# One-core hybrid decoder layer: key/value weights and transposed x loaded as one tile per k step, and three places re-ordered

## The chip, the cores and the metric

The kernel runs on one core of a Trainium2 chip. The metric is device time in microseconds (us), the median over runs of the same kernel. The engines are TensorE (PE: matmuls, PEld: its weight loads), VectorE (DVE), ScalarE (ACT), GpSimd (POOL) and SyncE (SP, which issues most DMA transfers). Each engine works its own queue of instructions in order and waits on semaphores of the others.

## The reference

One decoder layer in fp32, 256 tokens by 2048 channels, for batch 1 and depth 1:

```python
h = rmsnorm(x, norm_mix_pre[l])
proj = h @ w_in[l]
xr, yr, q, k, v, g_rnn, g_attn = jnp.split(proj, IN_OFFSETS, axis=-1)
xr = causal_depthwise_conv(xr, conv_w[l], conv_b[l])
xr = rg_lru(xr, positions, w_rg_a[l], b_rg_a[l], w_rg_x[l], b_rg_x[l], lru_lambda[l])
y_rnn = xr * jax.nn.gelu(yr)
q = rope(q.reshape(B, S, N_Q_HEADS, HEAD_DIM), positions)
k = rope(k.reshape(B, S, N_KV_HEADS, HEAD_DIM), positions)
v = v.reshape(B, S, N_KV_HEADS, HEAD_DIM)
y_att = sliding_window_sink_attention(q, k, v, attn_sinks[l])
mix = jax.nn.sigmoid(g_rnn) * (y_rnn @ w_rnn_proj[l]) + jax.nn.sigmoid(g_attn) * (y_att @ w_attn_proj[l])
x = x + rmsnorm(mix @ w_out[l], norm_mix_post[l])
h = rmsnorm(x, norm_mlp_pre[l])
u = jnp.square(jax.nn.relu(h @ w_mlp_up[l]))
x = x + rmsnorm(u @ w_mlp_down[l], norm_mlp_post[l])
```

There are 32 query heads and 4 key/value heads of 64 channels, so k and v together are 512 columns, and the MLP is 8192 wide. Attention runs in blocks of 128 tokens: the first block sees 128 keys, the second 256, under a mask and with one sink logit per head.

## The kernel before

Every matmul is built from three: each fp32 operand is split into a high part, which ACT casts (`hi`, `whi`), and a low part, which DVE subtracts (`lo`, `wlo`), and the products high x high, high x low and low x high are summed in one PSUM bank (128 x 512). One 512-wide product of the emulated kind is thus three matmuls of 512 columns.

Weights come through the class `Stream`. SP loads them in order as halves of 128 x 1024 (512 KB) into a ring of four tiles (`wraw`, WRAW = 4). ACT's cast and DVE's subtraction write rings of six (`whi`, `wlo`, WHALF = 6), and the matmuls take the halves by `half()`, which also keeps loads and splits a fixed number of halves ahead. For some pairs of halves, `SEVEN`, the MLP uses seven products over sums of blocks instead of eight. The Tile framework puts semaphores between engines; `pin` keeps marked instructions in program order, and the rest is scheduled by priority.

**Opening.** The program order of the loads is `w_kv` (8 halves, two k tiles of 512 columns each) mixed with x transposed (`x_t`: 256, 256 and three times 512 KB) on SP, and a small tile of constants `tiny` (105 KB, with the norm's gain `gcol`) on ACT's queue. Ten halves (`EXTRA`) lie in larger tiles of a pool with twelve places, so that 14 halves are loaded before any place in the ring must come free: the eight of `w_kv` and six of the gates. `split_first` splits the first half in two pieces; `part(k)` makes the high part of x times gain on ACT and the low part on DVE; `kv_step(j)` issues the matmuls of two k tiles into two banks `kv` (L415). Ahead of it stand 20 warm-up matmuls (L396). The tokens' scaling by the norm is applied later. After the opening the gate weights `w_g` follow (PE `g`, L307 to L311).

**Attention.** Attention of a key/value group g is a generator that yields between its steps, and the matmul loops of other work (`a_pair`, `b_pass512`) take one step from it every so many matmuls (`pump`). Its steps are scores, mask, maxima, `exponents` (ACT, L610), `shares` (DVE, scaling, L620), `turn_probs` (transposes on PE, `pt`, L636; copies to SBUF on ACT, L638), and the products with v (`po`, L678). A bank pool has two banks; `pt` uses the pool `psm`. The last group (g = 3) runs beside the matmuls `ps` with `hT` (L267, L269).

**Second norm.** The output projection of two token blocks (tb) by four quarters q of 512 columns ends in `o` banks. `gained` (DVE, L924, and ACT's squares, L921) and `scaled` by the norm (DVE, L967) make `h`, whose quarters PE transposes (`ptr`, L973), ACT casts to the high part of `h2T` (L978) and DVE subtracts to its low part (L983). Between the transposes of the second block stand the first matmuls of the MLP's up-projection (L1027), four or six at a time. ACT's queue holds the splits of the first weight halves of that projection (L116) there.

**Close.** The down-projection `down` of the last quarter pair sums 16 pairs of halves in four banks for (tb, n) = (0,0), (0,1), (1,0), (1,1). Two pairs are held back (`held` = 2) and done bank by bank at the end (L1134), each followed by `finish`: a sum on DVE (L1269), a square with row sum on ACT (L1270), a product with the gain on DVE (L1271). After a token block's last bank come the reduction (L1275), the root, the reciprocal, four scalings added to x (L1283) and the output transfers (L1284).

## Time and profile before

| what | us |
|---|---|
| median of 3 runs (1502.19 to 1502.8) | 1502.19 |
| the profiled execution | 1502.42 |
| its span in the trace | 1500.6 |
| PE busy | 1485.3 |
| DVE busy | 1097.8 |
| ACT busy | 829.6 |
| first real matmul starts (L415) | 7.43 |
| last matmul starts | 1490.58 |
| last reduction starts (L1275) | 1493.29 |

The profiled execution took 1.82 us more than its span, and 0.23 more than the median. The mean granted clock of PE over the span is 0.997 of full speed. DMA moved 199 GB/s over the span on the mean, and 339 in the first fortieth of it. A row of waits gives the engine and line that waited, what released it, the total in us, the number of times and the longest; a row of the timeline gives start, duration, engine, line, operation, tiles, count, and in square brackets the idle time before it and what ended it.

### The profile page before, as it was taken

Reading aid. Unit: us, or ns where it says so; the run is one execution under the profiler, and the core shown is the slowest. Engines: PE = TensorE matmul, PEld = TensorE weight load, DVE = VectorE, ACT = ScalarE, POOL = GpSimd, SP = SyncE. Lnnn points to the kernel's source line nnn. Section 1 sums busy time; section 2 is a strip of 40 time slices with the busy share of each in tenths; the row PEclk is TensorE's granted clock in tenths of the full one; section 3 lists DMA queues with packets and bytes.
Section 4 is the critical chain, followed back from the end, with each engine's and each line's share of the span. In section 5 each row is a group of like instructions: output and inputs, shape, how many; then the busy total and the mean of one; then the engine's idle time right before and its main releaser. Section 6 shows DMA issues by size and latency. Waiting matters only on the chain.

```text
span 1500.6 us, 19926 instructions
## 1 busy us (share of the span) xinstructions
PE 1485.3 (99%) x7568; PEld 1259.0 (84%) x7568; DVE 1097.8 (73%) x1356; ACT 829.6 (55%) x1137; POOL 1.7 (0%) x9
## 2 busy tenths in 40 slices
PE   9999999999999999999999999999999999999997
PEld 7887788788889888888889888888888888888886
DVE  6576668859669966555658866798886666788897
ACT  7564665647567665444355654555454555455453
POOL 0000000000000000000000000000000000000000
PEclk9999999999999999999999999999999999999999
DMA  8654554565646556555764765566667555566665
GB/s 339 217 161 156 166 163 136 169 195 172 210 155 211 179 200 208 184 191 188 276 216 144 262 190 192 186 208 206 210 204 242 189 193 187 192 239 210 204 215 186
DMA packets 83471, 298.28 MB, mean 199 GB/s; under 512 B 9264, under 2 KB 9520, under 8 KB 82352
## 3 DMA queue, kind: packets, MB, share of 16 engines
q1 hardware_dynamic: 80064, 289.57, 58.2%
q10 hardware_dynamic: 3312, 7.45, 1.4%
q8 instruction: 59, 0.97, 0.3%
q14 instruction: 36, 0.29, 0.1%
HBM read 290.69 MB, written 6.29 MB: 198 GB/s over the span
## 4 chain that ended last, share of the span: by engine, by line
PE 97%; DVE 2%; DMA 0%; ACT 0%; issue 0%; DVEq 0%; SPq 0%; ACTq 0%
PE ps L269 22%; PE ps L267 12%; PE dQ L1134 9%; PE s L1134 5%; PE dP L1134 4%; PE g L307 4%; PE g L311 4%; PE g L309 4%; PE pp L309 4%; PE pp L307 4%; PE pp L311 4%; PE dCs L1134 3%; PE q L307 2%; PE q L311 2%; PE q L309 2%; PE o L307 2%
## 5 line engine op out<-in xcount | busy, mean ns | idle before, releaser
L108 DVE TENSOR_TENSOR wlo<-wraw,whi 128x1024 fp32r<-128x1024 f32 x516 | 625.2, 1222 | 309.0 <-ACT whi L107 305.8
L107 ACT CAST whi<-wraw 128x1024 fp32r<-128x1024 f32 x516 | 537.8, 1051 | 546.5 <-PE ps L269 129.7
L269 PE MATMUL ps<-h2T,whi 128*128 128x512 f32 x960 | 223.9, 390 | 0.0
L269 PEld LDWEIGHTS ps<-h2T,whi 128*128 128x128 f32 x960 | 178.2, 188 | 35.7
L267 PEld LDWEIGHTS ps<-h2T,wlo 128*128 128x128 f32 x960 | 119.1, 192 | 2.3
L269 PE MATMUL ps<-hT,whi 128*128 128x512 f32 x512 | 120.7, 391 | 0.0
L267 PE MATMUL ps<-h2T,wlo 128*128 128x256 f32 x960 | 119.9, 283 | 0.0
L269 PEld LDWEIGHTS ps<-hT,whi 128*128 128x128 f32 x512 | 94.8, 188 | 20.3 <-issue 1.5
L1134 PE MATMUL dQ<-whi,uT 128*128 128x512 f32 x288 | 106.8, 389 | 0.0
L307 PE MATMUL g<-whi,hT 128*128 128x512 f32 x256 | 101.1, 395 | 0.0
L311 PE MATMUL g<-whi,hT 128*128 128x512 f32 x256 | 99.8, 390 | 0.0
L309 PE MATMUL g<-wlo,hT 128*128 128x512 f32 x256 | 99.8, 390 | 0.0
L267 PEld LDWEIGHTS ps<-hT,wlo 128*128 128x128 f32 x512 | 63.7, 192 | 1.2
L267 PE MATMUL ps<-hT,wlo 128*128 128x256 f32 x512 | 64.4, 283 | 0.0
L1134 PEld LDWEIGHTS dQ<-whi,uT 128*128 128x128 f32 x288 | 54.1, 188 | 11.2
L307 PEld LDWEIGHTS g<-whi,hT 128*128 128x128 f32 x256 | 48.1, 188 | 10.6 <-issue 1.0
L311 PEld LDWEIGHTS g<-whi,hT 128*128 128x128 f32 x256 | 48.0, 188 | 10.2
L309 PEld LDWEIGHTS g<-wlo,hT 128*128 128x128 f32 x256 | 48.1, 188 | 9.6
L1134 PE MATMUL dQ<-wlo,uT 128*128 128x512 f32 x144 | 56.0, 389 | 0.0
L1134 PE MATMUL dP<-whi,uT 128*128 128x512 f32 x144 | 54.1, 389 | 0.0
L1134 PE MATMUL dCs<-whi,uT 128*128 128x512 f32 x144 | 54.1, 389 | 0.0
L143 DVE TENSOR_TENSOR tlo<-t,thi 128x1536 fp32r<-128x1536 f32 x28 | 49.2, 1757 | 6.4 <-ACT thi L142 5.9
(284 smaller groups left out, 2464.5 us busy)
## 6 DMA issues: line engine op xcount, KB each, us to landing
wraw<-in_w_up SPq DMA_DIRECT2D x128, 512.0 KB, 4.1
wraw<-in_w_dn SPq DMA_DIRECT2D x128, 512.0 KB, 4.6
wraw<-in_w_g SPq DMA_DIRECT2D x64, 512.0 KB, 4.6
wraw<-in_w_xy SPq DMA_DIRECT2D x64, 512.0 KB, 4.6
wraw<-in_w_q SPq DMA_DIRECT2D x32, 512.0 KB, 4.4
wraw<-in_w_ap SPq DMA_DIRECT2D x32, 512.0 KB, 4.5
wraw<-in_w_rp SPq DMA_DIRECT2D x32, 512.0 KB, 3.8
wraw<-in_w_out SPq DMA_DIRECT2D x32, 512.0 KB, 5.1
```

The source lines that it names most:

```text
L107: self.pin(self.nc.scalar.copy(hi, src))
L108: self.pin(self.nc.vector.tensor_tensor(lo, src, hi.bitcast(F32), ALU.subtract))
L143: v.tensor_tensor(lo, t, hi.bitcast(F32), ALU.subtract)
L267: mm(ps[:, f, 1, :], w, a[:, 0, :], start=False, stop=j == 1 and k == 7)
L269: mm(ps[:, f].rearrange("p a b -> p (a b)"), w, a.rearrange("p a b -> p (a b)"), start=kt == 0, stop=j == 3 and k == 7)
L307: mm(banks[tb][n], a[:, 0, t], hi[:, n * 512 : n * 512 + 512], start=first, stop=False)
L309: mm(banks[tb][n], a[:, 0, t], lo[:, n * 512 : n * 512 + 512], start=False, stop=False)
L311: mm(banks[tb][n], a[:, 1, t], hi[:, n * 512 : n * 512 + 512], start=False, stop=last)
L1134: mm(b, a[x], w[y], start=not begun and i == 0, stop=tail and i == 2)
```

## The change

Four parts.

1. The opening. The key/value weights of one k tile (512 columns), x transposed of the same k tile (256), and, for the first, the norm's gain (16) lie side by side in memory, and each k tile is one transfer on SP: `kx_first` of 128 x 784 and fifteen `kx_rest` of 128 x 768. `tiny` goes to SP's queue behind the sixth. The split is per k tile (`kv_step(kt, hi, lo)`): a cast of 128 x 512 on ACT, of the first tile on DVE, the high and low part of x, the subtraction of 128 x 512, six matmuls. The stream's numbering starts at half 8 (`FIRST`), its large tiles are gone, so four gate halves are loaded before a place in the ring must come free, and not six.
2. Attention of the last group. One `yield` between its scores and masks, and one between the two `turn_probs(1, ...)`, are gone, one is added behind them; the transposes of the second pair part use the pool `psb`.
3. The second norm. `gained(1, 3)` and `scaled(1, 3)` come after `low(1, 0)`, and the third weight split of the up-projection after `high(1, 0)`.
4. The close. In the last `down` (`closing`) one more pair is worked first for the two banks of tb 0 only; its products for tb 1 are done at the end with the held pairs. The last bank (1,1) is done in two halves of 256 columns, the second in the free bank P1, with a fold of the partial sum on DVE (`fold`), and `finish` per half; sums of squares get five columns (`sq3`). The four scalings of tb 0 all come after (0,1), where before two came there and two after (1,0).

```diff
-EXTRA = 5
+FIRST = 8
...
-            if j < 2 * EXTRA:
-                if j % 2 == 0:
-                    self.place = self.room(f"wraw{j}")
-                t = self.place[:, c]
-            else:
-                t = self.pool.tile([P, 1024], F32, tag="wraw", bufs=WRAW, name=f"wraw{j}")
+            t = self.pool.tile([P, 1024], F32, tag="wraw", bufs=WRAW, name=f"wraw{j}")
...
+    kx, at = [], 0
+    for k in range(KT):
+        if k % 2 == 0:
+            place, at = flat(unit(f"kx{k}", F32)), 0
+        n = 512 + S + (KT if k == 0 else 0)
+        kx.append(place[:, at : at + n])
+        at += n
+        nc.sync.dma_start(kx[k], kx_rest[k - 1] if k else kx_first)
+        if k == 5:
+            nc.sync.dma_start(tiny, few)
+    gcol = kx[0][:, 512 + S :]
+    ws.load_to(FIRST + WRAW)
...
+    def kv_step(kt, hi, lo):
+        c, src = quarter(kt % 2), kx[kt][:, 0:512]
+        if kt:
+            pin(nc.scalar.copy(hi[:, c], src))
+        else:
+            pin(nc.vector.tensor_copy(hi[:, c], src))
+        part(kt)
+        pin(nc.vector.tensor_tensor(lo[:, c], src, hi[:, c].bitcast(F32), ALU.subtract))
+        for x, w in ((0, hi), (1, hi), (0, lo)):
+            for tb in range(TB):
+                pin(mm(kv[tb], hT[kt // 4][:, kt % 4, x, tb * P : tb * P + P], w[:, c],
+                       start=kt == 0 and w is hi and x == 0, stop=kt == KT - 1 and w is lo))
...
-                    ps = bank(psm, "pt")
+                    ps = bank(psb if last_group and tb and par else psm, "pt")
...
             three = scores(1, 1, [bank(psb, "sc") for par in range(2)])
-            yield
...
         turn_probs(1, (0,))
-        yield
+        if not last_group:
+            yield
         turn_probs(1, (1,))
         yield
+        if last_group:
+            yield
...
-    norm(1, lambda: low(0, 3), lambda: gained(1, 3, banks[1][1]))
-    for j in range(3):
+    norm(1, lambda: low(0, 3))
+    for j in range(2):
         begun.append(ws.split_high())
...
         high(1, q)
+        if q == 0:
+            begun.append(ws.split_high())
         low(1, q)
+        if q == 0:
+            gained(1, 3, banks[1][1])
+            scaled(1, 3)
...
+        def step(p, i, hi, lo, name, at=0, w=512, into=None):
+            tb, n2 = name
+            b = into or PLACE[name]
+            o = 0 if into else at
+            t = slice(tb * P, tb * P + P)
+            c = slice(n2 * 512 + at, n2 * 512 + at + w)
+            a = uT[p][:, i]
+            product(banks[b][:, o : o + w], (a[:, 0, t], a[:, 1, t]), (hi[:, c], lo[:, c]), b in begun,
+                    p == PAIRS - 1 and i == 1, w < 512 and not into)
+            begun.add(b)
...
+        if closing:
+            for i in range(2):
+                parts.append((PAIRS - held - 1, i) + ws.half())
+                for name in order[:2]:
+                    step(*parts[i], name)
...
+            if closing and k == 1:
+                a, r = order[-1], slice(256, 512)
+                fold = lambda: pin(v.tensor_tensor(ready[a][:, r], banks[PLACE[a]][:, r], ready[a][:, r], ALU.add))
+                for e in todo:
+                    step(*e, name)
+                finish(name, b, t, 0, 512, fold)
+            elif closing and k == 3:
+                for e in todo:
+                    step(*e, name, 0, 256)
+                finish(name, b, t, 0, 256)
+                for e in todo:
+                    step(*e, name, 256, 256, "P1")
+                finish(name, banks["P1"], t, 256, 256)
...
+            p = slice(at, at + w)
+            k = q + (at > 0)
+            pin(nc.vector.tensor_tensor(a[:, p], b[:, 0:w], t[:, p], ALU.add))
+            pin(nc.scalar.activation(spare[:, p], a[:, p], AF.Square, accum_out=sq3[:, tb, k : k + 1]))
+            pin(nc.vector.tensor_tensor(t[:, p], a[:, p], g3[:, q * 512 + at : q * 512 + at + w], ALU.mult))
             last[tb, i] = t
+            fold()
+            if at + w < 512:
+                return
...
-            for tb, qs in {(0, 1): ((0, (2, 0)),), (1, 0): ((0, (1, 3)),), (1, 1): ((1, (2, 0, 1, 3)),)}.get(name, ()):
+            for tb, qs in {(0, 1): ((0, (2, 0, 1, 3)),), (1, 1): ((1, (2, 0, 1, 3)),)}.get(name, ()):
```

At the opening, ACT's queue before, from its first transfer on (`wraw_80` holds w_kv, `xt_76` transposed x):

```order
L350 DMA tiny<-in_few 128x210
L377 ACT_TABLE_LOAD
L377 ACTIVATE st<-eps 128x1
L73 CAST whi_159<-wraw_80 128x512
L402 ACTIVATE hT_147<-xt_76,tiny 128x256
L73 CAST whi_159<-wraw_80 128x512
L402 ACTIVATE hT_147<-xt_76,tiny 128x256 x3
L116 CAST whi_185<-wraw_80 128x1024
L402 ACTIVATE hT_148<-xt_76,tiny 128x256 x2
L116 CAST whi_205<-wraw_86 128x1024
```

And ACT's queue after (`kx_77` holds k tiles 0 and 1):

```order
L350 ACT_TABLE_LOAD
L350 ACTIVATE st<-eps 128x1
L376 ACTIVATE hT_150<-kx_77 128x256
L385 CAST whi_162<-kx_77 128x512
L376 ACTIVATE hT_150<-kx_77 128x256
L385 CAST whi_184<-kx_80 128x512
L376 ACTIVATE hT_150<-kx_80,kx_77 128x256
L385 CAST whi_184<-kx_80 128x512
```

The first weight cast and the transfer of `tiny` have left ACT's queue, so that ACT begins with x; casts and parts of x now alternate one k tile at a time.

In the last group's attention, PE's queue before (`pt` is a transpose, L267 low and L269 high matmuls):

```order
L267 MATMUL ps<-hT_149,wlo_2311 128x256 x4
L267 MATMUL ps<-hT_150,wlo_2311 128x256 x4
L636 MATMUL pt<-ident,s 128x128 x8
L269 MATMUL ps<-hT_147,whi_2296 128x512 x3
...
L269 MATMUL ps<-hT_150,whi_2385 128x512 x4
L636 MATMUL pt<-ident,s 128x128 x8
L269 MATMUL ps<-hT_147,whi_2422 128x512
L267 MATMUL ps<-hT_147,wlo_2346 128x256 x4
L267 MATMUL ps<-hT_148,wlo_2346 128x256 x4
L267 MATMUL ps<-hT_149,wlo_2386 128x256
L636 MATMUL pt<-ident,s 128x128 x8
L267 MATMUL ps<-hT_149,wlo_2386 128x256 x3
```

And after (L248 low, L250 high matmuls, L609 transposes):

```order
L248 MATMUL ps<-hT_150,wlo_2217 128x256 x4
L248 MATMUL ps<-hT_151,wlo_2217 128x256 x4
L609 MATMUL pt<-ident,s 128x128 x8
L248 MATMUL ps<-hT_152,wlo_2283 128x256 x4
...
L248 MATMUL ps<-hT_153,wlo_2332 128x256 x4
L250 MATMUL ps<-hT_150,whi_2317 128x512 x3
L250 MATMUL ps<-hT_151,whi_2317 128x512 x4
L250 MATMUL ps<-hT_152,whi_2331 128x512 x4
L250 MATMUL ps<-hT_153,whi_2331 128x512 x4
L609 MATMUL pt<-ident,s 128x128 x16
L250 MATMUL ps<-hT_150,whi_2376 128x512 x4
```

The first eight transposes have moved ahead of 24 low matmuls, and the other two groups of eight, which had 10 matmuls between them, stand together.

In the second norm, DVE's queue before (L924 gains, L967 scalings, L983 low parts, L124 weight subtractions):

```order
L967 SCALAR_TENSOR_TENSOR h_6168<-h_6168,st,xg_6166 128x512 x3
L924 TENSOR_TENSOR h_6168<-o_6491,gpg_6160 128x512
L967 SCALAR_TENSOR_TENSOR h_6168<-h_6168,st,xg_6166 128x512
L983 TENSOR_TENSOR h2T_6177<-ptr_6753,h2T_6177 128x4x128
L983 TENSOR_TENSOR h2T_6178<-ptr_6754,h2T_6178 128x4x128
L124 TENSOR_TENSOR wlo_6874<-wraw_6676,whi_6820 128x1024
L983 TENSOR_TENSOR h2T_6179<-ptr_6753,h2T_6179 128x4x128
L983 TENSOR_TENSOR h2T_6180<-ptr_6754,h2T_6180 128x4x128
```

And after (L899, L932, L958, L105 in the same roles):

```order
L932 SCALAR_TENSOR_TENSOR h_6189<-h_6189,st,xg_6187 128x512 x3
L958 TENSOR_TENSOR h2T_6198<-ptr_6774,h2T_6198 128x4x128
L899 TENSOR_TENSOR h_6189<-o_6512,gpg_6181 128x512
L932 SCALAR_TENSOR_TENSOR h_6189<-h_6189,st,xg_6187 128x512
L958 TENSOR_TENSOR h2T_6199<-ptr_6775,h2T_6199 128x4x128
L105 TENSOR_TENSOR wlo_6895<-wraw_6697,whi_6839 128x1024
L958 TENSOR_TENSOR h2T_6200<-ptr_6774,h2T_6200 128x4x128
L958 TENSOR_TENSOR h2T_6201<-ptr_6775,h2T_6201 128x4x128
```

The first low part of block 1 stands ahead of the gain and the scaling of quarter 3, which before stood ahead of it.

More of the change, by code (lines that the diff above doesn't have):

```diff
@@ L60, in __init__ @@
         self.raw, self.parts = {}, {}
[L61 removed]
+        self.loaded = self.split = self.at = FIRST
         self.pin = lambda i: i
         self.high = []
[L64 to L77 removed]
     def load_to(self, n):
@@ L455, in sines @@
             nc.vector.tensor_scalar(ss[:, :, i, :], sn, 1.0 - 2.0 * i, None, ALU.mult)
-    ws.split_first(part)
-    kv_step(0)
     angle = angles()
-    for j in range(1, 8):
-        for i in range(2):
-            part(2 * j + i)
-        ws.split_high()
-        ws.split_low()
-        kv_step(j)
-        if j > 3:
+    for kt in range(KT):
+        if kt % 2 == 0:
+            halves = [wpool.tile([P, 1024], F32R, tag=tag, bufs=WHALF, name=f"{tag}{kt // 2}") for tag in ("whi", "wlo")]
+        kv_step(kt, *halves)
+        if kt > 8 and kt % 2:
             next(angle, None)
@@ L959, in norm @@
         pin(nc.scalar.activation(b, a, AF.Sqrt, bias=eps, scale=1.0 / D))
-        if between:
-            between()
+        between()
         pin(nc.vector.reciprocal(a, b))
-        for q in range(4):
-            c = quarter(q)
-            if q == 3 and late:
-                late()
-            pin(nc.vector.scalar_tensor_tensor(h2[tb][:, c], h2[tb][:, c], a, xg[tb][:, c], ALU.mult, ALU.add))
         r1.append(a)
+        for q in range(4 - tb):
+            scaled(tb, q)
     def turned(tb, q):
```

127 lines of the change are left out of this document (41 added, 86 removed).

## The prediction

> **What bounds the kernel now.** I read the page's busy times and its chain that ended last first, then the waits of the matmul engine (PE), then the places of those waits in the timeline.
>
> ```profile
> PE 1485.3 (99%) x7568; PEld 1259.0 (84%) x7568; DVE 1097.8 (73%) x1356; ACT 829.6 (55%) x1137; POOL 1.7 (0%) x9
> PE 97%; DVE 2%; DMA 0%; ACT 0%; issue 0%; DVEq 0%; SPq 0%; ACTq 0%
> ```
>
> ```profile
> PE kv L415 <- ACT hT L402: 2.5, 1, 2.5
> PE pt L636 <- ACT pT L638: 1.4, 1, 1.4
> PE ptr L973 <- DVE h2T L983: 0.7, 1, 0.7
> ```
>
> PE is busy 1485.3 of 1500.6 us, and the chain is 97% PE. So a reordering elsewhere is worth only the PE idle time it removes, the tail behind PE's last matmul, and any time in which PE runs at half clock. The waits of PE are three (total us, times, longest), one per place that the change touches: 2.5 us at the opening, 1.4 us in the last group's attention, 0.7 us in the second norm. Together 4.6 us; the rest is the close.
>
> The opening, from the chain and the timeline (start us, duration us):
>
> ```profile
> 1.17 5.61 DMA xt<-in_x_t
> 7.43 23.63 PE kv L415 x96
> 1479.41 3.40 PE dQ L1134 x15
> ```
>
> ```profile
> 0.74 0.38 SPq L89 DMA_DIRECT2D wraw<-in_w_kv  x1
> 1.08 3.85 PE L396 MATMUL warm<-ones 128*128 128x128 f32 x20 [1.08 <-DVE ones L380]
> 6.16 0.62 ACT L73 CAST whi<-wraw 128x512 fp32r<-128x512 f32 x1 [3.49 <-DMA wraw<-in_w_kv]
> 6.87 0.51 ACT L402 ACTIVATE hT<-xt,tiny 128x256 fp32r<-128x256 f32 x1
> ```
>
> Warm-up matmuls end at 4.93. The first weight half is there at 6.16, the first piece of transposed x at 1.17 + 5.61 = 6.78, and the first real matmul starts at 7.43. The 96 kv matmuls end at 7.43 + 23.63 = 31.06.
>
> The same stretch in windows (length; busy us of PE, PEld, DVE, ACT, POOL with counts; granted clock; DMA share; GB/s):
>
> ```profile
> 1.00:4.00 3.00, 2.92 (x14) 2.92 (x15) 0.03 (x1) 1.49 (x2) 1.23 (x4) 1.00 0.60 134
> 4.00:5.65 1.65, 0.93 (x9) 0.74 (x7) 0.00 (x0) 0.00 (x0) 0.00 (x0) 1.00 0.93 279
> 3.95:7.36 3.41, 0.98 (x9) 0.79 (x7) 0.00 (x0) 1.11 (x3) 0.00 (x0) 1.00 0.98 345
> 7.36:10.77 3.41, 3.34 (x8) 2.67 (x9) 3.36 (x7) 3.41 (x8) 0.00 (x0) 0.50 1.03 414
> 12.00:31.00 19.00, 19.00 (x85) 15.70 (x85) 16.68 (x33) 16.45 (x31) 0.00 (x0) 1.00 1.03 411
> 1488.70:1492.20 3.50, 2.27 (x11) 1.53 (x9) 3.46 (x6) 0.72 (x2) 0.00 (x0) 1.00 0.43 163
> ```
>
> Two things stand there. The DMA engines ramp: 134 GB/s until 4.0 us, then 279, then about 411. And from 7.36 to 10.77 PE is granted half its clock, just behind a stretch of the same length in which it was busy 0.98 of 3.41 us (29%). That costs about half of 3.41, 1.7 us. The sum agrees: a 512-wide matmul costs 3.40 / 15 = 0.227 us at full clock, so a k tile (six) 1.36 and the 96 of them 21.8 us; 23.63 are spent.
>
> **The opening, part by part.** Removed: 8 transfers of 512 KB, 5 of transposed x, the split in halves. Added: 16 transfers of a k tile (weights 512 columns, x 256, the first with the 16 gains: 128 x 784 x 4 = 401 KB, the rest 393 KB), all on SP's queue, the small constants behind the sixth. Bytes: 1.00 to 4.00 at 134 GB/s moved 402 KB, which is the whole first tile, where before the first half, `tiny` and the first x piece were 894 KB together (moved 402 + 1.65 x 279 = 862 KB by 5.65). x landed at 6.78, so landing comes about 1.15 us behind the last byte. The first tile then lands at 4.0 + 1.15 = 5.2. Earliest: 4.6, if the landing lag shrinks with fewer rows in flight. Latest: 6.16, where the first weight half landed with the same issue time. I take 5.2.
>
> Durations of the steps before the first matmul, from the groups by shape in 0 to 36 us (busy us, mean ns):
>
> ```profile
> L402 ACT ACTIVATE hT<-xt,tiny 128x256 fp32r<-128x256 f32 x16 | 7.2, 499 | 0.1
> L403 DVE SCALAR_TENSOR_TENSOR hT<-xt,tiny,hT 128x256 fp32r<-128x256 f32 x16 | 7.1, 481 | 6.4 <-ACT hT L402 6.4
> L75 DVE TENSOR_TENSOR wlo<-wraw,whi 128x512 fp32r<-128x512 f32 x2 | 1.4, 686 | 0.0
> L73 ACT CAST whi<-wraw 128x512 fp32r<-128x512 f32 x2 | 1.2, 609 | 3.5 <-DMA wraw<-in_w_kv 3.5
> ```
>
> For k tile 0 the high weights are now cast on DVE, and no row shows a DVE cast of that shape; between ACT's 0.61 and DVE's 0.69 for a subtraction of it I take 0.6. hT on ACT (0.50) runs beside. First matmul at 5.8 instead of 7.43. Its six: two at 5.8, two after DVE's hT (5.8 + 0.48 = 6.3), two after the low weights (6.3 + 0.69 = 7.0), done at 7.4. The second tile (795 KB in all) is moved by 5.5, landed 6.6; ACT casts (7.2) and makes hT (7.7); its last two matmuls wait for DVE (7.7 + 0.48 + 0.69 = 8.9) and end at 9.3. From then on a tile costs PE 1.36, ACT 0.61 + 0.50 = 1.11, DVE 0.48 + 0.69 = 1.17, DMA 393 KB / 411 = 0.96: PE is the slowest, so nothing else is late. End at 9.3 + 14 x 1.36 = 28.3, if the clock is full: 2.7 us before 31.06. Will it be? In 3.95 to 7.36 PE is then busy 0.98 + 1.35 = 2.3 us (68%). The one other part-idle stretch, 1488.70 to 1492.20 (2.27 of 3.50, 65%), had clock 1.00, and 29% brought the half clock; 68% is nearest the first. If the half clock stays, the tiles between 7.7 and 10.77 take double and kv ends at 29.6, gain 1.45.
>
> The Trainium skill, "TensorE: Matmul & The Clock Gate", section "What's actually happening", says the same length (3413 ns) and half clock after at least one idle window, but calls the window free-running, so that its phase varies between runs; the length agrees with the rows, the phase no run here shows. By that rule the 1.25 us between the two ends would come in some executions and not in others.
>
> Behind kv: only 4 gate halves are preloaded instead of 6 (the roomy tiles that held 10 halves are gone), so the fifth is loaded only when the first has been split.
>
> ```profile
> L108 DVE TENSOR_TENSOR wlo<-wraw,whi 128x1024 fp32r<-128x1024 f32 x516 | 625.2, 1222 | 309.0 <-ACT whi L107 305.8
> wraw<-in_w_g SPq DMA_DIRECT2D x64, 512.0 KB, 4.6
> ```
>
> DMA brings the tiles and 4 halves (8.5 MB, 0.86 of it by 5.65) by 24.2 us, then x by 29.3. PE starts the gates at 28.3 and takes 2.7 us per half (12 matmuls), so the fourth is wanted at 36.4 and the fifth at 39.2. DVE, free at 28, splits four at 1.22 each by about 33; the fifth, its place free at about 29.3, lands 4.6 later at 33.9, and is split by 36.3. Covered by some 3 us, cost nothing; if not, PE waits there (rival 3). Terms: opening −2.7, between −0.6 and −3.5.
>
> **Attention of the last group.**
>
> ```profile
> 266.02 4.00 PE L267 MATMUL ps<-hT,wlo 128*128 128x256 f32 x32
> 269.85 1.04 PE L636 MATMUL pt<-ident,s 128*128 128x128 f32 x8
> 280.88 1.05 ACT L638 COPY pT<-pt 128x512 f32<-128x512 f32 x2
> 281.51 1.14 PE L636 MATMUL pt<-ident,s 128*128 128x128 f32 x8 [1.39 <-ACT pT L638]
> ```
>
> The third eight transposes need the two banks that ACT copies out at 280.88 to 281.93, behind other ACT work. After, the first eight stand 24 low matmuls earlier (24 x 0.12 = 2.9 us, so at 267.0), and the other sixteen stand in one row, the second eight into the other bank pool: the wait for ACT's copies can't arise there. What is late next is the scaled probabilities, which DVE must have ready at 267.0 and at 274.1 (267.0 + 0.87 + 24 x 0.12 + 15 x 0.227). DVE's queue has the exponents of ACT ahead of these; moving the exponents ahead of the weight cast on ACT makes up about 1 us (a 128x1024 cast, less than twice the 0.61 of half its width). I put the new waits at 0.1 and 0.6: −1.4 + 0.7, about −0.6; from −1.4 (no new wait) to +0.3 (both DVE steps one 1.2 us subtraction later).
>
> **Second norm.**
>
> ```profile
> 803.78 2.93 ACT L116 CAST whi<-wraw 128x1024 fp32r<-128x1024 f32 x3
> 804.25 2.08 DVE L967 SCALAR_TENSOR_TENSOR h<-h,st,xg 128x512 f32<-128x512 f32 x3
> 805.22 0.60 PE L973 MATMUL ptr<-ident,h 128*128 128x128 f32 x4
> 806.36 0.60 PE L973 MATMUL ptr<-ident,h 128*128 128x128 f32 x4
> 807.63 1.28 DVE L983 TENSOR_TENSOR h2T<-ptr,h2T 128x512 fp32r<-128x512 f32 x2
> 808.37 0.66 PE L973 MATMUL ptr<-ident,h 128*128 128x128 f32 x4 [0.70 <-DVE h2T L983]
> ```
>
> Transposes come every 1.14 us (805.22, 806.36), so the third belonged at 807.50 and is 0.87 late: its bank is read by DVE only at 807.63, since ACT's third cast and DVE's two ops of q 3 (L924, L967) stand ahead. After, ACT has two casts (done 805.75), copies at 805.82 to 806.4, and DVE, free at 806.33, reads by 807.1: no wait at 807.50. The fourth is wanted at 808.65 plus four matmuls now ahead of it (0.5), 809.1; DVE does L924, L967 of q 3 (1.4) and the second read (0.7) by 809.2. −0.8; from −0.9 to −0.3 if the fourth waits.
>
> **Close.**
>
> ```profile
> 1490.58 0.39 PE L1134 MATMUL dQ<-whi,uT 128*128 128x512 f32 x1
> 1491.10 0.75 DVE L1283 SCALAR_TENSOR_TENSOR x<-t,st,x 128x512 f32<-128x512 f32 x1
> 1491.76 0.68 DVE L1269 TENSOR_TENSOR acc<-dQ,t 128x512 f32<-128x512 f32 x1
> 1492.54 0.63 ACT L1270 ACTIVATE spare<-acc 128x512 f32<-128x512 f32 x1 [1.93 <-DVE acc L1269]
> 1493.29 0.16 DVE L1275 TENSOR_REDUCE st<-sqs 128x1 f32<-128x4 f32 x1
> ```
>
> PE ends at 1490.97, but DVE is busy with the first half's scalings until 1491.8: the tail is DVE's. After, the last bank comes in two 256-wide halves: PE needs 36 x 0.12 instead of 18 x 0.227 (+0.2), and waits some 0.45 for the last low weights, which it reaches sooner. DVE gains a fold and splits two ops: about +0.6 by the 0.48 of a 128x256 op. The chain from the last sum to the reduction, 1.53 before, is half as wide: about 1.1. If DVE still sets it, the reduction moves from 1493.29 to 1493.5; if PE sets it (1491.65 + 1.1), to 1492.8. I take +0.1, from −0.7 to +0.7.
>
> **Sum.** −2.7 − 0.6 − 0.8 + 0.1 = −4.0 us. The profiled execution took 1502.42 (1.8 around the span), so 1498.4 for such a one; the median shown is 1502.19, so 1498.2.
>
> **Rivals.** 1. The half clock stays: opening −1.45, sum −2.75, 1499.4. For it: one threshold between 29% and 65% is all that the rows give. 2. The first tile lands at 6.16: PE at 6.8, gain about 0.6, 1500.3 with the half clock. 3. The smaller preload starves the gates' first halves and gives the opening back: −1.3, 1500.9. Against it: the 3 us of room above. 4, the other side: tiles of 393 KB come slower than PE eats them. Place: SP's queue, 5 to 31 us. PE is late above 1.36 us per tile; the whole change loses when kv ends after 32.4, tile 15 landing 15 tiles behind 5.2 and taking some 2.0 more: (32.4 − 7.2) / 15 = 1.68 us per tile, 234 GB/s. At 200 GB/s (1.97 per tile) kv ends at 36.7, 5.7 late, and the kernel takes 1502.2 − 1.3 + 5.7 = 1506.6. For it: 134 GB/s in the ramp; against it: 411 with pieces of 256 and 512 KB in one queue.
>
> The Trainium skill, "DMA: Bandwidth & Descriptors", section "Bandwidth", asks for 1 MiB or more per transfer to come to 75% of peak, and its fit (2.0 us plus bytes over 436 GB/s) gives an estimate of 2.9 us per tile; 16 in a row would be 46 us, some 16 us slower. The trace disagrees for transfers queued behind each other (411 GB/s at 256 and 512 KB), so it raises no chance of rival 4 beyond what follows.
>
> **Numbers.** A difference under 0.2% (3.0 us) can't be told from none. My forecast 0.62 (own range 1496.8 to 1499.4), rival 1 0.18, rival 2 0.06, rival 3 0.06, rival 4 0.08. Faster by over 3.0: 0.60 + 0.08 + 0.02 + 0.02 = 0.72; within: 0.02 + 0.10 + 0.04 + 0.04 = 0.20; slower: 0.08. Range: 1496.6 (attention and close at their low ends beside 28.3) to 1500.8 (rivals 1 and 2 in, 4 out).
>
> **What would show it.** First kv matmul near 5.8, clock 1.00 from 7.4 on, kv done near 28.3; no idle ahead of the first gate matmuls; the waits of PE without the 1.4 and 0.7, with new ones under 0.7 for the probabilities; the last reduction 1493.3 less 4. Wrong if the windows show half clock again, if kv waits for DMA after the second tile, or if PE waits at 31 to 45 us for gate weights.

## The result, and the profile after

The changed kernel takes 1496.12 us, the median of 5 runs (1495.96 to 1496.9), against 1502.19 before (1502.14 to 1503.18): 6.07 us or 0.4% less, ratio 0.9959 with a 95% interval of 0.9949 to 0.997. The forecast was 1498.2, a gain of 4.0, in a range from 1496.6: the sign was right, the gain was half as large again, and the time lies below the range. Two more times that the changed kernel was timed, beside runs of the kernel before of 1502.55 and 1502.56, it took 1495.57 and 1495.93. One run of the kernel before among the experiments, of 2128.03 us at a granted clock of 0.655, is left out of ratios and ranges.

The waits of PE in the changed kernel (total us, times, longest), and the kv matmuls in its chain of work:

```profile
PE warm L370 <- DVE ones L354: 1.1, 1, 1.1
PE pt L609 <- DVE s L593: 0.2, 1, 0.2
```

```profile
5.72 21.92 PE kv L392 x96
```

All three waits of before are gone (the 1.1 at the warm-up stood there before as well); 0.2 us is left in the attention, for the scaled probabilities. In the chain kv starts where the last warm-up ends, at 5.72, and it ends at 5.72 + 21.92 = 27.64 instead of 31.06. The opening's timeline:

```profile
2.74 2.98 PE L370 MATMUL warm<-ones 128*128 128x128 f32 x13
3.86 0.43 DVE L387 CAST whi<-kx 128x512 fp32r<-128x512 f32 x1 [2.83 <-DMA kx<-in_kx_first]
3.86 0.51 ACT L376 ACTIVATE hT<-kx 128x256 fp32r<-128x256 f32 x1 [1.63 <-DMA kx<-in_kx_first]
5.37 1.40 PE L392 MATMUL kv<-whi,hT 128*128 128x512 f32 x4
```

The first tile is there at 3.86, and cast and scaled at 4.4. PE doesn't start then: its warm-up matmuls still run, at 2.98 / 13 = 0.23 us each (0.213 from start to start), and the first kv matmul comes at 5.37. PE never waits for the opening's data in this profile (in `again`, the same kernel, it does for 0.3 us at the third tile). Its windows:

```profile
1.00:4.00 3.00, 2.92 (x13) 2.92 (x14) 0.17 (x2) 1.36 (x3) 1.23 (x4) 1.00 0.72 232
3.95:7.36 3.41, 3.41 (x17) 3.01 (x16) 2.51 (x5) 2.11 (x5) 0.00 (x0) 1.00 0.96 323
7.36:10.77 3.41, 3.41 (x17) 2.83 (x16) 2.62 (x6) 2.97 (x7) 0.00 (x0) 1.00 1.03 402
```

PE is busy throughout, and the transfers ramp faster than before (232 GB/s from 1 to 4 us, 134 before). The trace has the first release of the clock at 5.87 us, and the clock is not taken back behind it; the first kv matmuls still ran at half. The attention, the norm and the close (start, duration):

```profile
263.51 1.23 PE L609 MATMUL pt<-ident,s 128*128 128x128 f32 x8
271.50 1.75 PE L609 MATMUL pt<-ident,s 128*128 128x128 f32 x14 [0.24 <-DVE s L593]
```

```profile
801.91 0.60 PE L948 MATMUL ptr<-ident,h 128*128 128x128 f32 x4
803.06 0.60 PE L948 MATMUL ptr<-ident,h 128*128 128x128 f32 x4
804.74 0.66 PE L948 MATMUL ptr<-ident,h 128*128 128x128 f32 x4
```

```profile
1485.80 0.28 PE L1114 MATMUL s<-whi,uT 128*128 128x256 f32 x1
1486.12 0.42 DVE L1269 TENSOR_TENSOR acc<-s,t 128x256 f32<-128x256 f32 x1 [1.16 <-PE s L1114]
1487.12 0.16 DVE L1278 TENSOR_REDUCE st<-sq 128x1 f32<-128x5 f32 x1
```

The three rows of the norm are the second, third and fourth transposes: the third (803.06) come 1.15 us behind the second, without a wait, and the fourth have four more matmuls ahead of them than before. In the close DVE has been idle 1.16 us when PE delivers the last half bank: PE sets the end now. Place by place:

| place | before, us | after, us | change since the row above |
|---|---|---|---|
| last kv matmul ends | 31.06 | 27.64 | −3.4 |
| last matmul ends | 1490.97 | 1486.08 | −1.5 |
| last reduction starts | 1493.29 | 1487.12 | −1.3 |
| span ends | 1500.6 | 1493.7 | −0.7 |
| time of the execution | 1502.42 | 1495.96 | +0.4 |

The −1.5 are the attention (wait 1.39 to 0.24), the norm (0.7), and 0.4 lost. Of these, 0.2 are the close's narrow matmuls: 36 of 256 columns take PE 4.47 us, where 18 of 512 take 4.24 in the run `c_half` below. The other 0.2 have no place in the profile. The −0.7 behind the reduction come of the output's transfers, which nothing in the change touches; the last section returns to them.

### The profile page after: what moved, and what is told of

It is laid out like the page before. It is cut to its first block, busy times and chain, and to the rows that moved or that the text cites. A ratio compares the mean times of both kernels' runs of the same rounds, so it can differ in the third digit from the quotient of the medians.

```text
span 1493.7 us, 19993 instructions
## 1 busy us (share of the span) xinstructions
PE 1484.8 (99%) x7586; PEld 1259.8 (84%) x7586; DVE 1096.8 (73%) x1367; ACT 830.1 (56%) x1145; POOL 1.7 (0%) x9
## 4 chain that ended last, share of the span: by engine, by line
PE 98%; DVE 1%; ACT 1%; issue 0%; DVEq 0%; ACTq 0%
PE ps L250 21%; PE ps L248 11%; PE dQ L1114 9%; PE s L1114 5%; PE dP L1114 5%; PE g L288 4%; PE g L292 4%; PE g L290 4%; PE pp L290 4%; PE pp L292 4%; PE pp L288 4%; PE dCs L1114 3%; PE q L288 2%; PE q L292 2%; PE q L290 2%; PE o L290 2%
## 5 line engine op out<-in xcount | busy, mean ns | idle before, releaser
L250 PE MATMUL ps<-h2T,whi 128*128 128x512 f32 x960 | 224.0, 390 | 0.0
L250 PEld LDWEIGHTS ps<-h2T,whi 128*128 128x128 f32 x960 | 178.2, 188 | 35.7
L248 PEld LDWEIGHTS ps<-h2T,wlo 128*128 128x128 f32 x960 | 119.1, 192 | 2.3
L250 PE MATMUL ps<-hT,whi 128*128 128x512 f32 x512 | 120.6, 391 | 0.0
L248 PE MATMUL ps<-h2T,wlo 128*128 128x256 f32 x960 | 119.9, 283 | 0.0
L250 PEld LDWEIGHTS ps<-hT,whi 128*128 128x128 f32 x512 | 94.7, 188 | 19.5 <-issue 0.7
L1114 PE MATMUL dQ<-whi,uT 128*128 128x512 f32 (+1 forms) x288 | 105.3, 385 | 0.0
L248 PEld LDWEIGHTS ps<-hT,wlo 128*128 128x128 f32 x512 | 63.7, 192 | 2.1 <-issue 0.8
L248 PE MATMUL ps<-hT,wlo 128*128 128x256 f32 x512 | 64.6, 283 | 0.0
L1114 PE MATMUL dQ<-wlo,uT 128*128 128x512 f32 (+1 forms) x144 | 55.4, 385 | 0.0
L124 DVE TENSOR_TENSOR tlo<-t,thi 128x1536 fp32r<-128x1536 f32 x28 | 49.1, 1755 | 4.0 <-ACT thi L123 3.9
```

The costliest lines, as they stand in the source:

```text
L124: v.tensor_tensor(lo, t, hi.bitcast(F32), ALU.subtract)
L248: mm(ps[:, f, 1, :], w, a[:, 0, :], start=False, stop=j == 1 and k == 7)
L250: mm(ps[:, f].rearrange("p a b -> p (a b)"), w, a.rearrange("p a b -> p (a b)"), start=kt == 0, stop=j == 3 and k == 7)
L1114: mm(b, a[x], w[y], start=not begun and i == 0, stop=tail and i == 2, skip_group_check=shared)
```

## The experiments

Kernels that were timed as a group ran on one chip, each group beside the kernel before. Its medians in the four groups are 1503.22, 1502.55, 1502.76 and 1502.56 us.

**Each part put back.** The first group puts back one part at a time.

The opening (the other three parts stay):

```diff
-    for k in range(KT):
...
-        nc.sync.dma_start(kx[k], kx_rest[k - 1] if k else kx_first)
...
+    ws.load_to(1)
...
+    load_xt(0, 2)
...
+    ws.split_first(part)
+    kv_step(0)
```

> The changed kernel with the opening alone put back as it was before. Theory A (the two traces, place by place: opening 3.4 us, attention 1.0, norm 0.8, close 0.9): 1496.1 + 3.4 = 1499.5 us, kv done near 31.1 us, and half clock in the profile where the kernel before had it. Theory B (the sizes of the prediction, and the rest an accident of the profiled executions): 1496.1 + 2.7 = 1498.8 us. If the half clock of the kernel before was itself chance, its phase moves in this run, and the cost comes out between 1.7 and 3.4.

Measured: 1501.57 us (1498.94 to 1503.42, 11 runs), 5.4 above the changed kernel's 1496.1, and more than either theory gives. Its profile shows two things (kv matmuls; waits of PE):

```profile
7.22 2.07 PE L416 MATMUL kv<-whi,hT 128*128 128x512 f32 x4 [1.50 <-ACT hT L403]
9.10 1.05 PE L416 MATMUL kv<-wlo,hT 128*128 128x512 f32 x2
11.01 0.62 PE L416 MATMUL kv<-wlo,hT 128*128 128x512 f32 x2
```

```profile
PE dQ L1142 <- DVE wlo L108: 1.4, 2, 0.8
PE dQ L1142 <- DVE tlo L143: 0.8, 1, 0.8
```

kv runs at half clock until about 10 us (two matmuls in 1.05, later in 0.62) and ends at 30.67, 3.0 behind the changed kernel. Another 2.2 are waits for late weights near the end, in this execution, which took 1502.83. The changed kernel's profiles don't have them. So this run doesn't give the opening's price; it is taken up again below.

The attention:

```diff
-                    ps = bank(psb if last_group and tb and par else psm, "pt")
+                    ps = bank(psm, "pt")
...
             three = scores(1, 1, [bank(psb, "sc") for par in range(2)])
+            yield
...
         turn_probs(1, (0,))
-        if not last_group:
-            yield
+        yield
         turn_probs(1, (1,))
         yield
-        if last_group:
-            yield
```

> The changed kernel with the last group's attention put back. Theory A: 1496.1 + 1.0 = 1497.1 us, and PE waits 1.4 us for ACT's copies at the third group of transposes again. Theory B: 1496.1 + 0.6 = 1496.7 us.

Measured: 1497.05 us (1496.73 to 1498.69), 0.9 to 1.5 above the changed kernel's 1495.6 to 1496.1. Those come from other groups, and the kernel before is 0.5 to 0.7 slower in this one, so the size is good to some tenths only. The wait is back:

```profile
PE pt L609 <- ACT pT L611: 1.4, 1, 1.4
PE dQ L1112 <- DVE wlo L89: 0.8, 1, 0.8
```

Theory A, by the wait. The second row is a late weight in the close again, here in a kernel with the new opening. Of the profiles with the new close this one and `u_open` have it; what brings it isn't shown.

The norm:

```diff
-    norm(1, lambda: low(0, 3))
-    for j in range(2):
+    norm(1, lambda: low(0, 3), lambda: gained(1, 3, banks[1][1]))
+    for j in range(3):
         begun.append(ws.split_high())
...
-        if q == 0:
-            begun.append(ws.split_high())
         low(1, q)
-        if q == 0:
-            gained(1, 3, banks[1][1])
-            scaled(1, 3)
```

> The changed kernel with the second norm put back. Both theories: 1496.1 + 0.8 = 1496.9 us, and PE waits 0.7 us at the third transposes of token block 1. If the wait only moved further down, the time stays at 1496.1.

Measured: 1496.28 us (1495.92 to 1496.95), with the wait of 0.7 back in the profile. The changed kernel wasn't in this group, so a few tenths can't be read from it. The same kernel once more, beside the changed kernel:

> The changed kernel unaltered, as the yardstick on this call's chip for the kernel with the norm put back: 1496.0 us; kv done at 27.4 to 28.2, depending on when the clock is released.

> The changed kernel with the second norm put back, this time beside the changed kernel. Theory A: 0.7 to 0.8 us slower than it, as PE's wait of 0.7 us shows. Rival M (the time is taken back further down, since PE waits for something else less): 0.0 to 0.3 us.

Measured: 1495.93 us (1495.64 to 1496.72) for the changed kernel, 1496.72 (1496.29 to 1497.49) with the norm put back: 0.8 in the medians. The ranges of five runs each overlap a little, but the wait has the same size, 0.69, so rival M isn't borne out:

```profile
803.89 0.66 PE L948 MATMUL ptr<-ident,h 128*128 128x128 f32 x4 [0.69 <-DVE h2T L958]
```

The close:

```diff
...
-            for tb, qs in {(0, 1): ((0, (2, 0, 1, 3)),), (1, 1): ((1, (2, 0, 1, 3)),)}.get(name, ()):
+            for tb, qs in {(0, 1): ((0, (2, 0)),), (1, 0): ((0, (1, 3)),), (1, 1): ((1, (2, 0, 1, 3)),)}.get(name, ()):
...
-        down(f, n, uT, 2, [(0, 0), (0, 1), (1, 0), (1, 1)], finish, early, between, behind, True)
+        down(f, n, uT, 2, [(0, 0), (0, 1), (1, 0), (1, 1)], finish, early, between, behind)
```

The code for the deferred pair, the halves and the fold goes as well.

> The changed kernel with the close put back. Theory A: 1496.1 + 0.9 = 1497.0 us, DVE's last sum of 512 columns 0.8 us behind PE's end. Theory B (the close is worth nothing, as predicted): 1496.0 us.

Measured: 1496.95 us (1496.75 to 1497.68), 0.8 to 1.4 above the changed kernel in the other groups. Theory A; my +0.1 for the close falls. DVE's queue at the end, in that kernel:

```profile
1485.54 0.75 DVE L1262 SCALAR_TENSOR_TENSOR x<-acc,st,x 128x512 f32<-128x512 f32 x1
1486.20 0.75 DVE L1262 SCALAR_TENSOR_TENSOR x<-t,st,x 128x512 f32<-128x512 f32 x1
1486.86 0.68 DVE L1248 TENSOR_TENSOR acc<-dQ,t 128x512 f32<-128x512 f32 x1
1488.39 0.16 DVE L1254 TENSOR_REDUCE st<-sqs 128x1 f32<-128x4 f32 x1
```

Two scalings of block 0 stand ahead of the last sum, as before, and the reduction starts at 1488.39 rather than 1487.12, although PE's last matmul ends at 1486.08 in both kernels.

**The close taken apart.** First the halves alone taken back, then the scalings alone.

```diff
-            if closing and k == 1:
+            if False and k == 1:
...
-            elif closing and k == 3:
+            elif False and k == 3:
...
```

> The changed kernel unaltered, on the chip of this call, as the yardstick for the three others: 1496.1 us. If the kernel before is at 1503 here, the chip and not the change carries 1 us of it.

> The changed kernel with the last bank of the close in one piece of 512 columns, and without the fold; the later scalings and the deferred pair stay. Theory A, in its parts: DVE is free when PE ends, so 0.8 of the close stays gained, and the split gave 0.5 less 0.2 to 0.4 of PE time for the narrower matmuls: 1496.1 + 0.1 to 0.3. Rival: the split gives all 0.9, and 1497.0 is measured.

Measured side by side: 1495.57 us (1495.34 to 1497.15) for the changed kernel, 1495.92 (1495.4 to 1497.14) without halves. The ranges lie over each other, so the difference isn't told from none; the rival (all 0.9 from the split) falls.

```diff
-            for tb, qs in {(0, 1): ((0, (2, 0, 1, 3)),), (1, 1): ((1, (2, 0, 1, 3)),)}.get(name, ()):
+            for tb, qs in {(0, 1): ((0, (2, 0)),), (1, 0): ((0, (1, 3)),), (1, 1): ((1, (2, 0, 1, 3)),)}.get(name, ()):
```

> The changed kernel with the four scalings of token block 0 put back to two after bank (0,1) and two after bank (1,0); halves and fold stay. Theory A: DVE is then busy with two scalings (1.4 us) when PE delivers the last bank, the last reduction starts 1.5 to 2 us behind PE's end instead of 1.04, and 0.5 to 0.9 us are lost: 1496.5. Rival: DVE has 1.16 us idle there and takes them in, 0 to 0.2 us lost.

Measured: 1496.03 us (1495.15 to 1496.32), no loss against the 1495.6 to 1496.1 of the other groups; theory A fell in this, the rival holds. DVE ahead of the last sum, without halves and then with the scalings put back:

```profile
1485.71 0.69 DVE L1269 TENSOR_TENSOR acc<-dQ,t 128x512 f32<-128x512 f32 x1 [1.83 <-PE dQ L1114]
1487.26 0.16 DVE L1278 TENSOR_REDUCE st<-sq 128x1 f32<-128x4 f32 x1
```

```profile
1485.95 0.42 DVE L1269 TENSOR_TENSOR acc<-s,t 128x256 f32<-128x256 f32 x1 [0.76 <-PE s L1114]
1486.94 0.16 DVE L1278 TENSOR_REDUCE st<-sq 128x1 f32<-128x5 f32 x1
```

In both DVE waits for PE. Either edit, with the deferred pair of weights that both keep, is enough to take DVE off the end; the two don't add up. No run has the deferred pair alone, but these rows give an estimate: DVE is idle 1.83 us ahead of the last sum without the halves, and two scalings would take 1.4 of that. By this the deferred pair would do it by itself. It makes the last bank 18 matmuls long instead of 12, which gives DVE 6 x 0.227 = 1.4 us more before the last sum is due.

**The opening taken apart.** The kernel before with the new opening alone:

```diff
-    ws.split_first(part)
-    kv_step(0)
...
+    for kt in range(KT):
+        if kt % 2 == 0:
+            halves = [wpool.tile([P, 1024], F32R, tag=tag, bufs=WHALF, name=f"{tag}{kt // 2}") for tag in ("whi", "wlo")]
+        kv_step(kt, *halves)
```

> The kernel before with the new opening and nothing else. Theory A: 3.0 to 3.6 us off the kernel before in the trace (kv done at 27.4 to 28.2 instead of 31.1), so its median lies 3 to 4 us under that of the kernel before in this call. Theory G (putting the opening back cost 5.4 us in the earlier call, so it is worth more than its place in the trace shows): 5 us or more.

Measured: 1498.51 us (1498.16 to 1499.26, 9 runs) against 1502.76 before, ratio 0.9971 (0.9962 to 0.9981): 4.25 us, between the two theories. kv ends at 5.72 + 22.05 = 27.77, 3.3 ahead of the kernel before. The other 0.9 has its place too. From the last reduction to the end of the span it is 6.5 us here and 7.3 in the kernel before (the output's transfers, 0.8). The time around the span gives 0.2 back (medians of the runs 1.8 and 2.0). And the kernel before was 0.3 faster in its profiled execution than its median in this group.

```profile
5.72 22.05 PE kv L391 x96
```

The 1.2 us by which `u_open` lost more than this stay open; the late weights at the new close, 2.2 in its profile, go with them.

How fixed is the other side, the half clock of the kernel before? It ran once more, unaltered, for a second profile:

> The kernel before once more, for a second profile of its opening. Theory K (PE's idle 2.5 us meets the clock's window at another phase in each execution): full clock begins at another time than 3.94 us, half clock comes at another time or not at all, and kv ends between 29.5 and 31.5. If the phase is fixed by the program, the numbers repeat: 3.94, 7.36, 10.77 and 31.06.

Measured: 1502.54 us. Windows in the same form as before:

```profile
5.55:8.96 3.41, 1.74 (x7) 1.02 (x7) 1.61 (x4) 2.76 (x7) 0.00 (x0) 1.00 1.04 414
8.97:12.38 3.41, 3.41 (x10) 2.62 (x9) 3.35 (x7) 3.08 (x6) 0.00 (x0) 0.50 1.01 401
```

The half clock comes again, as long as before, but from 8.97 to 12.38 and not from 7.36 to 10.77; kv ends at 31.25. So in two executions its length is the same and its phase isn't, as theory K has it. The window ahead of it had PE busy for 1.74 of 3.41 us. In another thing this profile differs from the first: the DMA rate from 1 to 4 us is 164 GB/s and not 134. What PE's idle time has to do with it, the next run shows, the kernel before with longer warm-ups:

```diff
-WARM = 10
+WARM = 14
```

> The kernel before with 28 warm-up matmuls instead of 20 (WARM = 14), so that PE is busy until 6 to 7 us and waits under 1.5 us for the first tile. Theory K (the half clock from 7.36 to 10.77 came of the idle 2.5 us): full clock stays from its release on, kv is done at 29.3 to 29.8 instead of 31.06, and 1.0 to 1.7 us are gained on the kernel before. Rival L (the phase of the clock's window is chance, and the idle time has no part in it): the half clock may fall in 7 to 11 us all the same, and the median stays within 0.5 us.

Measured: 1501.41 us (1500.74 to 1502.03, 11 runs) against 1502.76, ratio 0.9993 (0.9985 to 1.0002).

```profile
6.64:10.05 3.41, 3.16 (x15) 2.18 (x15) 2.71 (x6) 3.32 (x8) 0.00 (x0) 1.00 1.03 391
```

```profile
7.36 22.27 PE kv L415 x96
```

PE's wait shrinks to 0.25, the clock stays, and kv ends at 29.63, 1.4 earlier, with its first matmul where it was (7.36). Theory K: 1.4 us of the opening are the clock's. The interval of the ratio reaches 1, so the median alone would not show it; the place does, and so does the spread: the eleven runs lie within 1.3 us, while those of the kernel before reach from 1500.75 to 1504.83. In the profiled execution only 0.7 of the 1.4 reaches the last reduction (1492.62 instead of 1493.29), since DVE sets the end of the old close.

Why did the first tile come at 3.86, and not at 5.2? Three runs. The small constants on ACT's queue at the start, as before:

```diff
+    nc.scalar.dma_start(tiny, few)
...
-        if k == 5:
-            nc.sync.dma_start(tiny, few)
```

> The changed kernel with the small constants (128 x 194) issued at the start on ACT's queue, as the kernel before did, instead of on SP behind the sixth tile. Theory C (their rows beside the first tile slow the ramp): the DMA rate from 1 to 4 us falls from 232 to about 134 GB/s, the first tile lands at 5.0 to 5.3 instead of 3.86; PE, whose warm-up matmuls last until 5.7, loses little, 0 to 0.5 us. Rival D (the tile lands early because it is one transfer of 401 KB at the head of the queue): 3.9 to 4.2 and no change of the time.

Measured: 1496.6 us (1496.21 to 1497.61), against 1495.57 (1495.34 to 1497.15) beside it: ranges that overlap. The first tile is there at 4.19, the rate is 218. Both lie within what the other profiles with this first transfer have (3.81 to 4.36 us, 206 to 235 GB/s), so theory C falls.

```profile
1.00:4.00 3.00, 2.92 (x13) 2.92 (x14) 0.03 (x1) 1.49 (x2) 1.24 (x4) 1.00 0.70 218
```

Two transfers per tile instead of one:

```diff
-        nc.sync.dma_start(kx[k], kx_rest[k - 1] if k else kx_first)
+        src = kx_rest[k - 1] if k else kx_first
+        for c in (slice(0, 512), slice(512, n)):
+            nc.sync.dma_start(kx[k][:, c], src[:, c])
```

> The changed kernel with every k tile fetched in two transfers, the 512 weight columns and then x (rows of 2 KB and 1 KB), 32 transfers instead of 16. Theory H (one transfer per tile is what makes the tiles early): SP issues one in about 0.43 us, so tile k is issued 0.43 later per tile, and smaller rows slow the rate; the first tile is whole at 4.3 to 4.8, kv is done 0.3 to 1.0 us later. Rival I (the order, a tile at a time, is all): first tile at 4.0, kv done as before within 0.3 us.

Measured: 1497.8 us (1497.25 to 1499.27, 7 runs), some 2 us slower than the changed kernel. Yet the first tile is whole at 3.75: its landing isn't the reason, and neither theory H nor rival I has the cause. The rate from 12 to 28 us is 372 GB/s (399 with one transfer), but PE is busy all of that time. It waits at two places farther down, the gates at 37 us and the up-projection at 824 us:

```profile
PE ps L250 <- DVE u L1058: 0.5, 1, 0.5
PE g L290 <- DVE wlo L89: 0.5, 1, 0.5
```

Of the 2.1 us by which the last reduction is later, the two waits are 1.0, and 0.5 is the end of kv, where the clock came at 6.93 us instead of 5.87. So one transfer per tile instead of two is worth something, and not by the first landing; that the rate is the reason is likely for the gates' wait alone and isn't shown for the rest. The third run gave the first transfer the shape of the first weight half before, rows of 4 KB out of 8 KB:

```diff
-        nc.sync.dma_start(kx[k], kx_rest[k - 1] if k else kx_first)
+        nc.sync.dma_start(kx[k], kx_rest[k - 1] if k else kx_first[:, 0:1024])
```

> The changed kernel with the first transfer shaped as the first weight half was before: 128 rows of 4 KB (784 numbers used, the rest zeros) out of rows of 8 KB, 512 KB in all. If size alone counts, it lands 0.12 MB later than the 401 KB tile at some 350 GB/s, at 4.2 us. Theory N (rows of 4 KB out of 8 KB come slowly while the DMA engines start): 5.0 us or later, with the rate from 1 to 4 us near the 134 of the kernel before instead of 213 to 235.

Measured: 1497.1 us, a single run.

```profile
1.00:4.00 3.00, 2.92 (x13) 2.92 (x14) 0.03 (x1) 1.22 (x2) 1.23 (x4) 1.00 0.68 170
```

```profile
5.37 0.43 DVE L387 CAST whi<-kx 128x512 fp32r<-128x512 f32 x1 [4.34 <-DMA kx<-in_kx_first]
5.95 1.24 PE L392 MATMUL kv<-whi,hT 128*128 128x512 f32 x4 [0.94 <-ACT hT L376]
```

It lands at 5.37, not at the 4.2 that its size would give, and PE waits 0.94 us. Theory N holds: the shape of the first transfer costs more than its bytes. The ramp's 170 GB/s stand next to the 161 to 164 of three of the four profiles with the old opening; the 134 came in one execution. Rows, strides and size weren't separated, so which of them it is stays open.

Last, fewer warm-ups in the changed kernel, since they keep PE past 4.4 us:

```diff
-WARM = 10
+WARM = 6
```

> The changed kernel with 12 warm-up matmuls instead of 20 (WARM = 6). Theory E (the warm-ups, at half clock until the release, keep PE busy past the landing of the first tile): they end at 3.7, the first kv matmul starts at 4.4 and not at 5.4, and the kernel gains 0.3 to 0.7 us: about 1495.6. Rival F (the warm-ups' time was needed to release the clock): the gap of PE before 4.4 puts the release off by a window, up to 1.7 us slower, 1497.5.

Measured: 1496.11 us (1496.01 to 1497.65) against 1495.57 for the changed kernel: no gain.

```profile
4.38 1.21 PE L392 MATMUL kv<-whi,hT 128*128 128x512 f32 x2 [0.37 <-ACT hT L376]
```

kv starts at 4.38 as expected, but at half clock (0.6 us per matmul) until the release at 6.15, and ends at 27.80, no earlier than with 20 warm-ups (27.40 to 28.22 in three profiles of the changed kernel). Theory E has the start right and the gain wrong; the loss of rival F didn't come either. What starts sooner runs slower here.

## Why the prediction fell short

The time fell below the range because terms were mis-sized on the same side: above all the opening (the landing of the first tile) and the close (which engine sets its end), and to a lesser part the attention.

**The reading of the bounds held.** PE set the end, and what was to be had were its waits, the half clock and the tail. What the kernel gained up to the last reduction came from there. No rival happened: no half clock behind the first release, no late tile, no wait for gate weights (rival 3's place, 31 to 45 us, has no PE wait), no DMA slower than PE.

**The landing of the first tile (step "first tile at 5.2") failed.** I took the rate of the kernel before, 134 GB/s until 4 us, for a property of the chip's start and applied it to another transfer. It wasn't even fixed for that kernel: its second profile has 164. The tile came at 3.86, at a rate of 232: `first4k` shows that the old shape brings the rate down to 170 and the landing to 5.37. My lower end, 4.6, was too late as well. The sizes behind it were also a little too long: DVE's cast took 0.43, not 0.6.

**The first matmul (5.8 told, 5.37 measured) was right by luck.** I had PE wait for the tile; in fact it was still at its warm-ups, which ran at half clock until the release at 5.87. In the profile before, where the release came at 3.95, they were over at 4.93.

**The clock.** "Full from 7.4 on" held, but not for my reason. I weighed a PE busy for 68% of a window against two rows; PE had no gap at all, and full clock began at 5.87 us, not at 3.95. Windows of the kernel with the opening put back, and of the one with the first transfer of 4 KB rows:

```profile
3.40:6.81 3.41, 2.32 (x11) 2.03 (x10) 0.00 (x0) 0.77 (x2) 0.00 (x0) 1.00 0.97 310
```

```profile
4.10:7.51 3.41, 2.47 (x14) 1.61 (x13) 1.51 (x3) 1.52 (x3) 0.00 (x0) 1.00 0.99 364
7.51:10.92 3.41, 3.41 (x16) 2.43 (x15) 3.24 (x7) 3.24 (x8) 0.00 (x0) 1.00 1.04 405
```

The first, ahead of any release, had PE busy for 2.32 of 3.41 us (68%), and its matmuls behind it ran at half clock until 10.2; the second, right behind a release, had 2.47 (72%), and the clock was kept. The windows at the ends of the kernels, counted from the release in steps of 3.41 us, tell more. Behind a release the clock was kept after every window with 1.83 us busy or more (54%, `u_close`) and lost after every one with 1.47 or less (43%, `u_att`). Between these both occur: it was lost after 1.74 (51%) in `b_again` and kept after 1.54 (45%) in `b_warm14`. So 68% behind a release would have been enough by these traces, and the busy time that a profile counts doesn't give a sharp limit. The Trainium skill, "TensorE: Matmul & The Clock Gate", section "What's actually happening", has the window free-running; the two profiles of the kernel before agree, with a shift of 1.6 us. The opening's term was mis-sized: −2.7 told, −3.4 by its place, −4.25 by the median of `open_only`. Of the 3.4, `b_warm14` gives 1.4 to the clock. The 2.0 that are left are the earlier start of kv in the chain (7.36 to 5.72, 1.6) and a shorter kv (22.27 to 21.92, 0.4).

**The attention (−0.6) was too cautious.** I set 0.7 us for new waits, and 0.24 came: the exponents moved ahead of the cast by enough. By the waits −1.15, by the run −0.9 to −1.5.

**The norm (−0.8) was right,** in size and place: third transposes without a wait (0.7 before), and 0.8 us in the median of `norm2`.

**The close (+0.1) failed in the step "If DVE still sets it".** I counted the extra ops on DVE (+0.6). I left nearly out of the sum that two scalings, 1.4 us, move out of its way, and that the deferred pair gives it 1.4 us more before the last sum is due. DVE was idle 1.16 us ahead of the last sum. `c_scal` shows that the scalings weren't needed for this, `c_half` that the halves weren't; the deferred pair, which both keep, is enough by the estimate above and was not run alone. The other branch that I wrote down, PE setting the end, was the right one; in it the chain from the last sum to the reduction was 1.0, as told (1.1). PE lost 0.2 on the narrow matmuls, as told, and the wait for the last weights (0.45 told) came in two profiles, as up to 0.8, in the others not.

**The sum.** −3.4 − 1.15 − 0.7 − 0.9 = −6.2 at the last reduction, where I had −4.0 (the −0.9 of the close are the tail's −1.3 with the 0.4 that PE lost). Three quarters of the missing 2.2 us are the close and the opening's first microseconds. The range's low end left no room for all terms being too cautious together; the same care (a late landing, new waits, a DVE-bound tail) went into each of them.

## What to carry to other kernels

A ramp, a landing lag or a half clock that a trace shows at the start belongs to the transfers and the idle time of that kernel, and in part to that execution (134 and 164 GB/s in two of the kernel before): don't carry it over to another first transfer as a constant. When two engines may set a tail, write the sum for both, and count what leaves the engine's queue, and the time that it gains before its last work is due, as carefully as what is added. And where each term is rounded to the careful side, the sum is biased; say for each whether its error is likely to have the same sign.

## What the runs showed of the hardware that I had not expected

The output's transfers (256 KB each) land faster in every kernel with the new opening, although nothing in them differs. From the list of transfers behind 1475 us, before and then after (KB each, median us from issue to landing):

```profile
out<-x SPq DMA_DIRECT2D x4, 256.0 KB, 2.5
out<-x ACTq DMA_DIRECT2D x4, 256.0 KB, 2.6
```

```profile
out<-x SPq DMA_DIRECT2D x4, 256.0 KB, 2.0
out<-x ACTq DMA_DIRECT2D x4, 256.0 KB, 2.1
```

All four profiles with the old opening have a median of 2.6 or 2.7, all fourteen with the new one 2.1 (in `apart` one of the eight took 2.8). The inputs in memory differ between the two, in number and size; whether that is the cause wasn't tried. The span became 0.7 to 0.8 us shorter by it, but the time around the span grew, from 1.8 us in the runs of the kernel before to 2.0 in those of `open_only` and 2.3 in those of the changed kernel (medians). So some 0.6 us of it are in the measured time of `open_only`, and 0.2 to 0.3 in that of the changed kernel. Why the time around the span grows isn't shown.

The first transfer's speed hangs on its shape: 401 KB in rows of 3 KB landed 3.1 us after its issue (3.1 to 3.6 in twelve profiles), 512 KB in rows of 4 KB out of 8 KB 4.6 us, in one, with the same work around them. The Trainium skill, "DMA: Bandwidth & Descriptors", section "Anatomy of one DMA — SWDGE (gpsimd) path", fits 2.0 us plus bytes over 436 GB/s to single transfers that GpSimd issues: for the first, from SP here, an estimate of 2.9, which is near, and for the second of 3.2, which isn't. Taken one by one for the sixteen tiles in one queue it doesn't hold: they came at about 400 GB/s.

The granted clock in the windows stands at 1.00 from the start, but before the first release PE runs at half: from start to start the warm-up matmuls took 0.21 us until then, and in the kernel before, whose release came ahead of their end, 0.11 behind it. The release came between 3.9 and 7.1 us in seventeen of the eighteen profiles, and at 10.2 in `u_open`. In the three profiles of the changed kernel it came at 4.59, 5.15 and 5.87.
